# Mixture-of-experts stage: a large and a small expert run as a pair, gate and up of both, then down of both

## The chip, the cores and the metric

One core of one Trainium2 chip runs the whole program. The metric is the device time of one execution in microseconds (us). TensorE (PE) multiplies, VectorE (DVE) and ScalarE (ACT) work on the results, GpSimd (POOL) does little here, SyncE (SP) issues the transfers from HBM, and DMA engines carry them. Every engine takes its own instructions in a written order and waits for the others through semaphores.

## The reference

Two layers of mixers and feed-forward over 256 context and 256 latent tokens of width 1024. The change lies in the feed-forward of the second layer, where each latent token goes to the best two of eight experts:

```python
def swiglu(h, w_gate, w_up, w_down):
    return (jax.nn.silu(h @ w_gate) * (h @ w_up)) @ w_down

def moe_swiglu(h, router_w, w_gate, w_up, w_down):
    logits = (h @ router_w).astype(F32)
    top_v, top_i = lax.top_k(logits, TOP_K)
    top_w = jax.nn.softmax(top_v, axis=-1)
    combine = jnp.sum(jax.nn.one_hot(top_i, N_EXPERTS, dtype=F32) * top_w[..., None], axis=-2)
    out = jnp.zeros(h.shape[:-1] + (w_down.shape[-1],), h.dtype)
    for e in range(N_EXPERTS):
        out = out + combine[..., e:e + 1].astype(h.dtype) * swiglu(h, w_gate[e], w_up[e], w_down[e])
    return out
```

D_MODEL is 1024, D_FF is 2816, all weights are float32: 33 MB (of 1,048,576 bytes) for one expert, 264 for the eight.

## The kernel before

The experts are sorted by the number of their tokens and paired, a large one (up to 128 tokens) with a small one (up to 64): slots 0 and 1, 2 and 3, and so on. An expert that has more tokens than its slot holds is finished by a path behind a branch at the end, which does not run here.

`gather` (L1145) picks the tokens of both experts of a pair by a matmul with a one-hot matrix `oh` and writes `xg` for the large and `xs` for the small one. `pick` (L1136) makes that matrix for the next pair. `scatter_rows` (L1160) turns it for the way back, and `scatter` (L1296) scales one half of an expert's output (`y`, L1300 on ACT and L1301 on DVE), multiplies it with the turned matrix and adds it to the stream `xl` (L1309). The scatter of the second half (`late`) is put off into the expert that follows.

`expert` (L1175) is the large one. Its weights come as 33 loads of 1 MB each, 22 for gate and up in six groups `g`, 11 for down. A weight tile is split into a high and a low part (`split`, L346): ACT writes `whi` (L352), DVE writes `wlo` (L353) from it; two pieces per load, three pairs of buffers. Three matmuls, high with high, high with the low part of the tokens, low with high (L1197 to L1199 for gate and up, L1233 to L1235 for down), stand for one in full precision. The activation of a group (L1202, L1203) is transposed on PE (L1208) in the middle of the next group. `expert64` (L1240) is the small one: its weights are not split, and two halves of the columns go through the array side by side (L1254). Its activation (L1260 on ACT, L1261 on DVE) is transposed (L1266) and copied (L1268, ACT); down is L1290. Four of the next pair's gathers and more stand between its down matmuls.

The loop at the end calls `expert(0)`, `expert64(1)`, `expert(2)` and so on, each with gate and up and then down. Loads are issued by SP in the program's order, as buffers come free; there are ten of them (three in `wpool`, four in `mo`, three of the freed tiles `own` and `whole`). The framework's scheduler sets the written order of each engine from the program's order, its priorities (splits have a high one) and the dependences. PSUM is cut into pools: `pj` three buffers, `pm` three, `po` and `pa` one each. Gate and up of the large expert take `po` and `pa` in even groups and `pj` in odd ones, the small one takes `pj`; down accumulates in two buffers of `pm`, from which transposes, gathers and scatters are served too.

The entries of `PLAN` that matter: `sg` (group after which the scatter rows are made), `tt` and `td` (where in the next group, and in down, a transpose is called), `pk` (after which group `pick` is called), `gd` (first down load with a gather), `sd` (down load after which the first half is scattered).

Of the kernel before, what the change touches and what calls it, by code (L numbers as in the profile page):

```python
# [83 lines left out]
def host_layout(x, c, ctx, c_ctx, ada_w, ada_b, mix_norm_w, ffn_norm_w, w_in, hg_lb_logits, hg_norm_w,  # L84
# [97 lines left out]
    "ff": (1, 1),  # L182
    "sg": 1,
    "tt": 2,
    "td": 2,
    "slots": (3, 5, 8),
    "pk": 3,
    "gd": 1,
    "sd": 8,
    "dv": ([], [4, 5, 6, 7, 8, 9, 10, 11, 12, 13, 14, 15, 16, 17, 18]),  # L190
# [8 lines left out]
def tile_kernel(ctx: ExitStack, tc: tile.TileContext, xT, cT, cR, ada_w, w_in, w_br, w_out, ffn_gu, ffn_d, router,  # L199
# [975 lines left out]
    def expert(e, oh, st, choose, early):  # L1175
        pr, ee = divmod(e, 2)
        at_ = home_of(e)
        if ee:
            return expert64(e, at_, oh, st, choose, early)
        xv = [xg[:, s_] for s_ in range(2)]  # L1180
        aT, turn_ = [], []
        for g in range(6):
# [3 lines left out]
            for u in range(2):  # L1186
                ps = pj() if g % 2 else pt(("po", "pa")[u], 1)
                for c in range(8 // kc):
                    n = 4 * g + 2 * u + c if g < 5 else 20 + u
                    raw = load(moe[at_, n]).rearrange("p (k c) -> p k c", k=kc)  # L1190
                    for k0 in range(0, kc, kc // 2):
                        if turn_ and 4 * (kc * c + k0) >= kc * PLAN["tt"]:
                            turn_.pop()()
                        hi, lo = split(raw[:, k0:k0 + kc // 2], (kc // 2, w))
                        for k in range(kc // 2):
                            kk = kc * c + k0 + k
                            T.matmul(ps[:, :w], xv[0][:, kk], hi[:, k], start=kk == 0, stop=False)  # L1197
                            T.matmul(ps[:, :w], xv[1][:, kk], hi[:, k], start=False, stop=False)  # L1198
                            T.matmul(ps[:, :w], xv[0][:, kk], lo[:, k], start=False, stop=kk == 7)  # L1199
# [15 lines left out]
            if g == PLAN["pk"]:  # L1215
                choose()
            if g == PLAN["sg"]:
                if late:
                    late.pop()()
                st.update(zip(("ws", "oT"), scatter_rows(pr, oh)))  # L1220
        pd = [pm(), pm()]
        for c in range(11):
            raw = load(moe[at_, 22 + c]).rearrange("p (k c) -> p k c", k=4)
            early(c - PLAN["gd"])
            for k in range(4):
                h_, kk = DOWN[4 * c + k]
                if turn_ and 4 * c + k == 2 * PLAN["td"]:
                    turn_.pop()()
                if k % 2 == 0:
                    hi, lo = split(raw[:, k:k + 2], (2, 512))  # L1230
                ahi, alo = (x[:, kk % 4] for x in aT[kk // 4])
# [4 lines left out]
            if c == PLAN["sd"]:  # L1236
                scatter(e, 0, pd[0], st["ws"], st["oT"])
        late.append(lambda: scatter(e, 1, pd[1], st["ws"], st["oT"]))

    def expert64(e, at_, oh, st, choose, early):  # L1240


        aT, turn_ = {}, []
        for g in range(6):
# [3 lines left out]
            for u in range(2):  # L1248
                for c in range(8 // kc):
# [7 lines left out]
                    if turn_:  # L1257
                        turn_.pop()()
# [15 lines left out]
            if g == PLAN["pk"]:  # L1274
                choose()
            if g == PLAN["sg"] and late:
# [3 lines left out]
        pd = [pm(), pm()]  # L1280
        for c in range(11):
            raw = load(moe[at_, 22 + c]).rearrange("p (k c) -> p k c", k=4)
            early(c - PLAN["gd"])
            for k in range(4):
                h_, kk = DOWN[4 * c + k]
                if turn_ and c == 1:
                    turn_.pop()()
# [4 lines left out]
            if c == PLAN["sd"]:  # L1292
                scatter(e, 0, pd[0], st["ws"], st["oT"])
        late.append(lambda: scatter(e, 1, pd[1], st["ws"], st["oT"]))
# [26 lines left out]
    late, ohs = [], [pick(0)]  # L1321
    for k in range(KD):
        gather(k, ohs[0], True)
    for pr in range(4):
        st = {}
        for ee in range(2):
            def choose():
                if ee and pr < 3:
                    ohs.append(pick(pr + 1))

            def ahead(k):
                if ee and pr < 3 and 0 <= k < KD:
                    gather(k, ohs[pr + 1], False)

            expert(2 * pr + ee, ohs[pr], st, choose, ahead)
    late.pop()()
# [109 lines left out]
```

## Time and profile before

| what | us |
|---|---|
| median of 3 runs (2147.19 to 2152.62) | 2149.67 |
| profiled execution | 2153.76 |
| its span on the core | 2151.9 |
| PE busy in the span | 2065.4 |
| DVE busy | 1304.0 |
| ACT busy | 926.7 |

All durations of instructions come from the one profiled execution. A matmul's row lasts longer than the step to the next matmul, because matmuls overlap; a step is read from two starts. The expert stage begins with the first large matmul at 1449.8 us and reaches to 2144 us, and a pair takes about 175 us. In the windows below, 1716.4 to 1763.6 us is gate and up of the second small expert, and 1763.6 to 1790.4 us its down.

### The profile page before, as it was taken

How to read it: one execution, taken by the hardware profiler on the slowest of the kernel's cores; microseconds unless marked ns; L12 is line 12 of the kernel's file. 1: busy time of each engine (PE TensorE's matmuls, PEld its weight loads, DVE VectorE, ACT ScalarE, POOL GpSimd, SP SyncE). 2: the span in 40 equal slices, each digit the busy share in tenths (PEclk: the TensorE clock that was granted, in tenths of full speed). 3: DMA queues.
4: the chain of work that ended last, by engine and by line, in shares of the span. 5: the costliest groups of instructions: out<-in, count | busy, mean ns of one | idle time of the engine just before them, and what ended most of it. 6: DMA issues, size and time to landing. Idle time of an engine off the chain costs nothing.

```text
span 2151.9 us, 34449 instructions
## 1 busy us (share of the span) xinstructions
PE 2065.4 (96%) x13828; PEld 1580.3 (73%) x13828; DVE 1304.0 (61%) x2362; ACT 926.7 (43%) x1423; POOL 35.3 (2%) x101
## 2 busy tenths in 40 slices
PE   6999999999999999999999999989999999999997
PEld 3777777777867878887778878878757856865863
DVE  7677456664455468634777777669618806915931
ACT  3653233322334222223755443448527616815731
POOL 0001000010000000000000000000000000000000
PEclk9999999999999999999999999989999999999999
DMA  8341413112263346421333222469999999999996
GB/s 322 128 157 61 172 64 118 40 61 79 100 233 118 113 163 243 157 67 61 126 128 118 99 102 80 147 245 335 365 422 420 385 419 416 371 397 420 375 392 247
DMA packets 66983, 455.46 MB, mean 212 GB/s; under 512 B 7680, under 2 KB 8192, under 8 KB 13952
## 3 DMA queue, kind: packets, MB, share of 16 engines
q1 hardware_dynamic: 64224, 447.78, 53.9%
q10 hardware_dynamic: 2592, 5.41, 0.8%
q8 instruction: 111, 1.82, 0.3%
q14 instruction: 56, 0.46, 0.1%
HBM read 452.11 MB, written 1.05 MB: 211 GB/s over the span
## 4 chain that ended last, share of the span: by engine, by line
PE 90%; DVE 4%; ACT 3%; DMA 2%; issue 1%; SPq 0%; DVEq 0%; ACTq 0%
PE pj L359 15%; PE pj L361 15%; PE pj L360 15%; PE pj L1254 7%; PE pm L1290 4%; PE pm L1235 2%; PE pm L1233 2%; PE pm L1234 2%; PE pj L1197 2%; PE pj L1198 2%; PE pj L1199 2%; PE pm L596 1%; PE pa L803 1%; PE pm L379 1%; PE po L1199 1%; PE po L1197 1%
## 5 line engine op out<-in xcount | busy, mean ns | idle before, releaser
L352 ACT ACTIVATE whi<-raw 128x1024 fp32r<-128x1024 f32 (+3 forms) x442 | 436.4, 993 | 579.4 <-PE pj L360 504.9
L353 DVE TENSOR_TENSOR wlo<-raw,whi 128x1024 fp32r<-128x1024 f32 (+3 forms) x442 | 497.8, 1140 | 214.6 <-ACT whi L352 203.5
L359 PE MATMUL pj<-hhi,whi 128*128 128x512 f32 (+1 forms) x1216 | 452.0, 373 | 9.9 <-ACT hhi L488 9.0
L361 PE MATMUL pj<-hhi,wlo 128*128 128x512 f32 (+1 forms) x1216 | 450.7, 371 | 0.4 <-DVE wlo L353 0.4
L360 PE MATMUL pj<-hlo,whi 128*128 128x512 f32 (+1 forms) x1216 | 449.7, 370 | 0.2 <-DVE hlo L489 0.2
L359 PEld LDWEIGHTS pj<-hhi,whi 128*128 128x128 f32 x1216 | 230.1, 189 | 51.9 <-ACT hhi L488 11.8
L361 PEld LDWEIGHTS pj<-hhi,wlo 128*128 128x128 f32 x1216 | 229.9, 189 | 40.6 <-issue 5.4
L360 PEld LDWEIGHTS pj<-hlo,whi 128*128 128x128 f32 x1216 | 230.3, 189 | 39.3 <-issue 3.0
L1254 PE MATMUL pj<-raw,whole 128*64 128x256 f32 (+1 forms) x1088 | 114.4, 362 | 0.0
L1261 DVE TENSOR_TENSOR act<-act,pj 128x256 f32<-128x256 f32 (+1 forms) x24 | 9.6, 399 | 156.6 <-ACT act L1260 156.6
L1254 PEld LDWEIGHTS pj<-raw,whole 128*64 128x64 f32 x1088 | 73.5, 137 | 33.2 <-issue 2.2
L1260 ACT ACTIVATE act<-pj 128x256 f32<-128x256 f32 (+1 forms) x24 | 8.8, 367 | 144.2 <-PE pj L1254 144.2
L359 PE MATMUL pj<-yhi,whi 128*128 128x512 f32 (+1 forms) x192 | 66.8, 350 | 3.4 <-ACT yhi L514 3.1
L361 PE MATMUL pj<-ahi,wlo 128*128 128x512 f32 x176 | 69.3, 394 | 0.5 <-DVE wlo L353 0.5
L359 PE MATMUL pj<-ahi,whi 128*128 128x512 f32 x176 | 69.0, 392 | 0.0
L1233 PE MATMUL pm<-whi,ahi 128*128 128x512 f32 x176 | 69.0, 392 | 0.0
L1198 PE MATMUL pj<-whi,xg 128*128 128x512 f32 (+1 forms) x192 | 68.9, 359 | 0.0
L360 PE MATMUL pj<-alo,whi 128*128 128x512 f32 x176 | 68.6, 390 | 0.0
L1234 PE MATMUL pm<-whi,alo 128*128 128x512 f32 x176 | 68.6, 390 | 0.0
L1197 PE MATMUL pj<-whi,xg 128*128 128x512 f32 (+1 forms) x192 | 68.4, 356 | 0.2 <-ACT whi L352 0.2
L1235 PE MATMUL pm<-wlo,ahi 128*128 128x512 f32 x176 | 68.2, 390 | 0.0
L1199 PE MATMUL pj<-wlo,xg 128*128 128x512 f32 (+1 forms) x192 | 68.0, 354 | 0.0
(362 smaller groups left out, 3620.0 us busy)
## 6 DMA issues: line engine op xcount, KB each, us to landing
raw<-in_moe_dram SPq DMA_DIRECT2D x185, 1024.0 KB, 8.8
raw<-in_w_in_dram SPq DMA_DIRECT2D x58, 1024.0 KB, 4.8
own<-in_moe_dram SPq DMA_DIRECT2D x53, 1024.0 KB, 8.9
raw<-in_ada_w_dram SPq DMA_DIRECT2D x44, 1024.0 KB, 4.9
whole<-in_moe_dram SPq DMA_DIRECT2D x26, 1024.0 KB, 8.1
raw<-in_ffn_gu_dram SPq DMA_DIRECT2D x22, 1024.0 KB, 4.9
raw<-in_w_br_dram SPq DMA_DIRECT2D x12, 1024.0 KB, 4.8
raw<-in_ffn_d_dram SPq DMA_DIRECT2D x16, 704.0 KB, 4.1
```

Source lines behind the costliest of these rows:

```text
L352: S.activation(hi, src, AF.Copy)
L353: V.tensor_tensor(lo, src, hi.bitcast(F32), ALU.subtract)
L359: T.matmul(ps, whi(k), hhi(k), start=first and k == 0, stop=False)
L360: T.matmul(ps, whi(k), hlo(k), start=False, stop=False)
L361: T.matmul(ps, wlo(k), hhi(k), start=False, stop=last and k == n - 1)
L1197: T.matmul(ps[:, :w], xv[0][:, kk], hi[:, k], start=kk == 0, stop=False)
L1198: T.matmul(ps[:, :w], xv[1][:, kk], hi[:, k], start=False, stop=False)
L1199: T.matmul(ps[:, :w], xv[0][:, kk], lo[:, k], start=False, stop=kk == 7)
L1233: T.matmul(pd[h_], ahi, hi[:, k % 2], start=first, stop=False)
L1234: T.matmul(pd[h_], alo, hi[:, k % 2], start=False, stop=False)
L1235: T.matmul(pd[h_], ahi, lo[:, k % 2], start=False, stop=last)
L1254: T.matmul(ps[64 * h_:64 * h_ + 64, u, :hw], xs[:, kk], raw[:, k, h_ * hw:(h_ + 1) * hw], start=u + kk == 0, stop=u == 1 and kk == 7, tile ...
```

## The change

Both functions become generators. `expert` and `expert64` no longer run to their end: they give back control after each group of gate and up and after each load of down. A new function `pair` calls them in turn. In pair 0 a string gives the order of the groups: three large, six small, three large; in the other pairs six large, then six small. After that come the 11 down loads of the large expert, then the 11 of the small one. The list of transposes to be made, `turn_`, is now one for both. Down accumulates in `po` and `pj` (large) and `pa` and `pj` (small) instead of `pm`. The late scatter of the large expert falls into small down, that of the small expert still into the next pair's gate and up. `pk` counts the groups of both experts, and `td` is gone.

```diff
     "tt": 2,
-    "td": 2,
     "slots": (3, 5, 8),
-    "pk": 3,
+    "pk": 8,
     "gd": 1,
     "sd": 8,
+    "first": "BBBSSSSSSBBB",
...
-    def expert(e, oh, st, choose, early):
-        pr, ee = divmod(e, 2)
+    turn_, late = [], []
+
+    def do_turn():
+        if turn_:
+            turn_.pop()()
+
+    def expert(e):
...
-                        if turn_ and 4 * (kc * c + k0) >= kc * PLAN["tt"]:
-                            turn_.pop()()
+                        if 4 * (kc * c + k0) >= kc * PLAN["tt"]:
+                            do_turn()
...
-            if g == PLAN["pk"]:
-                choose()
-            if g == PLAN["sg"]:
-                if late:
-                    late.pop()()
-                st.update(zip(("ws", "oT"), scatter_rows(pr, oh)))
-        pd = [pm(), pm()]
+            yield
+        pd = [None, None]
         for c in range(11):
             raw = load(moe[at_, 22 + c]).rearrange("p (k c) -> p k c", k=4)
-            early(c - PLAN["gd"])
             for k in range(4):
                 h_, kk = DOWN[4 * c + k]
-                if turn_ and 4 * c + k == 2 * PLAN["td"]:
-                    turn_.pop()()
+                if c == 1 and k == 0:
+                    do_turn()
...
+                if pd[h_] is None:
+                    pd[h_] = pj() if h_ else pt("po", 1)
...
-            if c == PLAN["sd"]:
-                scatter(e, 0, pd[0], st["ws"], st["oT"])
-        late.append(lambda: scatter(e, 1, pd[1], st["ws"], st["oT"]))
+            yield pd
...
-    def expert64(e, at_, oh, st, choose, early):
+    def expert64(e):
...
-                    if turn_:
-                        turn_.pop()()
+                    do_turn()
...
         for c in range(11):
             raw = load(moe[at_, 22 + c]).rearrange("p (k c) -> p k c", k=4)
-            early(c - PLAN["gd"])
+            do_turn()
             for k in range(4):
                 h_, kk = DOWN[4 * c + k]
-                if turn_ and c == 1:
-                    turn_.pop()()
+                if pd[h_] is None:
+                    pd[h_] = pj() if h_ else pt("pa", 1)
...
+    def pair(pr):
+
+        both = expert(2 * pr), expert64(2 * pr + 1)
+        for n, who in enumerate(PLAN["first"] if pr == 0 else "B" * 6 + "S" * 6):
+            next(both["BS".index(who)])
+            if n == PLAN["sg"]:
+                if late:
+                    scatter(*late.pop())
+                rows = scatter_rows(pr, ohs[pr])
+            if n == PLAN["pk"] and pr < 3:
+                ohs.append(pick(pr + 1))
+        for ee in range(2):
+            e = 2 * pr + ee
+            for c in range(11):
+                pd = next(both[ee])
+                if c == PLAN["sg"] and late:
+                    scatter(*late.pop())
+                if c == PLAN["sd"]:
+                    scatter(e, 0, pd[0], *rows)
+                if ee and pr < 3 and 0 <= c - PLAN["gd"] < KD:
+                    gather(c - PLAN["gd"], ohs[pr + 1], False)
+            late.append((e, 1, pd[1], *rows))
...
     for pr in range(4):
-        st = {}
-        for ee in range(2):
-            def choose():
-                if ee and pr < 3:
-                    ohs.append(pick(pr + 1))
-
-            def ahead(k):
-                if ee and pr < 3 and 0 <= k < KD:
-                    gather(k, ohs[pr + 1], False)
-
-            expert(2 * pr + ee, ohs[pr], st, choose, ahead)
-    late.pop()()
+        pair(pr)
+    scatter(*late.pop())
```

In the kernel after, the lines of the large expert are L1202 to L1204 (gate and up), L1213 (its transpose) and L1234 to L1236 (down); of the small one L1254 as before, L1259 (activation), L1265 (transpose), L1267 (copy) and L1286 (down). In the scalings L1294 stands for L1300.

ACT, at the end of the second pair's small gate and up (`act` is the activation, `whole` holds the copies of the transposes, `x` and `xg` belong to the gathers). Before:

```order
L1268 ACTIVATE whole<-pm_15674 128x256
L1260 ACTIVATE act_15696<-pj_15655 128x128
L1156 ACTIVATE x_15714<-pm_15709,mods_145,coef_149 128x128
L1156 ACTIVATE whole<-pm_15709,mods_145,coef_149 128x64
L1157 ACTIVATE xg_13119<-x_15714 128x128
L1268 ACTIVATE whole<-pm_15719 128x128
L1156 ACTIVATE x_15732<-pm_15727,mods_145,coef_149 128x128
```

Now, at the same place:

```order
L1267 ACTIVATE whole<-pm_15399 128x256
L1259 ACTIVATE act_15421<-pj_15381 128x128
L1267 ACTIVATE whole<-pm_15449 128x128
L352 ACTIVATE whi_15426<-raw_15424 128x1024
L352 ACTIVATE whi_15437<-raw_15424 128x1024
L352 ACTIVATE whi_15452<-raw_15447 128x1024
```

The splits of the large expert's down weights follow the small expert's last copy directly, where the gathers stood.

PE at the same place. Before, small gate and up is followed by small down and gathers, with the last transpose among them:

```order
L1254 MATMUL pj_15655<-raw_15656,whole 64x128 x16
L1254 MATMUL pj_15655<-raw_15678,whole 64x128 x16
L1290 MATMUL pm_15699<-raw_15701,whole 64x512 x4
L1148 MATMUL pm_15709<-oh_15604,hn_2117_13065 128x192 x2
L1148 MATMUL pm_15709<-oh_15604,hn_2118_13066 128x192 x2
L1266 MATMUL pm_15719<-cc,act_15696 128x128
L1290 MATMUL pm_15699<-raw_15707,whole 64x512 x4
```

Now it is followed by the transpose and then by large down:

```order
L1254 MATMUL pj_15381<-own,whole 64x128 x16
L1254 MATMUL pj_15381<-raw_15403,whole 64x128 x16
L1265 MATMUL pm_15449<-cc,act_15378 128x128
L1234 MATMUL po_15430<-whi_15426,ahi_14638 128x512
L1235 MATMUL po_15430<-whi_15426,alo_14639 128x512
L1236 MATMUL po_15430<-wlo_15427,ahi_14638 128x512
```

The transpose stands right behind its group, and the first large matmuls need the split parts `whi` and `wlo`.

ACT at the end of the last pair's small gate and up, where L1279 (now L1275) has a table of functions loaded. Before:

```order
L1260 ACTIVATE act_18368<-pj_18327 128x128
ACT_TABLE_LOAD
L1279 ACTIVATE most_18371<-act_18368 128x1
L1268 ACTIVATE whole<-pm_18382 128x128
L1300 ACTIVATE y_18429<-pm_18373,ws_17415 128x512
```

Now:

```order
L1259 ACTIVATE act_18093<-pj_18052 128x128
ACT_TABLE_LOAD
L1275 ACTIVATE most_18357<-act_18093 128x1
L352 ACTIVATE whi_18098<-raw_18096 128x1024
L352 ACTIVATE whi_18109<-raw_18096 128x1024
L1267 ACTIVATE whole<-pm_18120 128x128
L352 ACTIVATE whi_18123<-own 128x1024
```

Two splits stand ahead of the last copy here, behind the table and L1275.

## Rows read from the trace of the kernel before

**Rows 1.** The page's busy time, share and instructions of PE; shares of the ending chain:

```profile
PE 2065.4 (96%) x13828; PEld 1580.3 (73%) x13828; DVE 1304.0 (61%) x2362; ACT 926.7 (43%) x1423; POOL 35.3 (2%) x101
...
PE 90%; DVE 4%; ACT 3%; DMA 2%; issue 1%; SPq 0%; DVEq 0%; ACTq 0%
```

**Rows 2.** Windows: length, busy time (instructions) PE, PEld, DVE, ACT, POOL, PEclk, DMA share, GB/s:

```profile
1449.80:1619.40 169.60, 165.73 (x993) 118.70 (x992) 96.53 (x116) 88.61 (x122) 0.00 (x0) 0.99 0.94 369
1619.40:1792.10 172.70, 165.69 (x1001) 119.09 (x1001) 98.88 (x117) 89.36 (x120) 0.00 (x0) 1.00 1.00 409
...
1716.40:1763.60 47.20, 42.50 (x405) 28.19 (x406) 4.52 (x10) 4.53 (x11) 0.00 (x0) 1.00 1.00 408
1763.60:1790.40 26.80, 26.70 (x131) 10.55 (x125) 5.04 (x14) 8.75 (x27) 0.00 (x0) 1.00 1.01 420
```

**Rows 3.** Waits of PE, 1450 to 2144 us: total, times, longest us:

```profile
PE pm L1266 <- DVE act L1261: 16.0, 17, 0.9
PE po L1197 <- ACT whi L352: 5.2, 3, 1.7
PE po L1199 <- DVE wlo L353: 1.6, 3, 0.5
...
```

**Rows 4.** Timeline, first small to large turn: start, length, engine, line, operation, idle before:

```profile
1615.80 1.89 PE L1290 MATMUL pm<-whole 128*64 128x512 f32 x8
...
1617.73 0.69 ACT L1300 ACTIVATE y<-pm,ws 128x512 fp32r<-128x512 f32 x1 [5.67 <-PE pm L1290]
1618.32 2.94 ACT L352 ACTIVATE whi<-raw 128x1024 fp32r<-128x1024 f32 x3
...
1619.40 3.49 DVE L353 TENSOR_TENSOR wlo<-raw,whi 128x1024 fp32r<-128x1024 f32 x3 [0.19 <-ACT whi L352]
...
1619.42 0.50 PE L1197 MATMUL po<-whi,xg 128*128 128x512 f32 x1 [1.73 <-ACT whi L352]
...
1620.68 0.50 PE L1199 MATMUL po<-wlo,xg 128*128 128x512 f32 x1 [0.53 <-DVE wlo L353]
...
1621.01 0.39 PE L1197 MATMUL po<-whi,xg 128*128 128x512 f32 x1
...
1621.24 0.39 PE L1198 MATMUL po<-whi,xg 128*128 128x512 f32 x1
```

**Rows 5.** Timeline, end of the last small gate and up:

```profile
2107.65 0.42 DVE L1261 TENSOR_TENSOR act<-act,pj 128x256 f32<-128x256 f32 x1 [8.01 <-ACT act L1260]
2108.12 0.44 PE L1266 MATMUL pm<-cc,act 128*128 128x128 f32 x2 [0.94 <-DVE act L1261]
...
2112.03 1.89 PE L1290 MATMUL pm<-own,whole 128*64 128x512 f32 x8
2112.25 0.28 ACT L1260 ACTIVATE act<-pj 128x128 f32<-128x128 f32 x1 [3.27 <-PE pj L1254]
2112.56 0.29 DVE L1261 TENSOR_TENSOR act<-act,pj 128x128 f32<-128x128 f32 x1 [4.49 <-ACT act L1260]
2113.84 0.20 ACT L1279 ACTIVATE most<-act 128x1 f32<-128x1 f32 x1 [1.31 <-DVE act L1261]
2113.85 0.33 PE L1266 MATMUL pm<-cc,act 128*128 128x128 f32 x1
...
2114.22 0.28 ACT L1268 ACTIVATE whole<-pm 128x128 f32<-128x128 f32 x1 [0.17 <-PE pm L1266]
```

**Rows 6.** Windows behind the three turns (columns as in rows 2):

```profile
1793.40:1796.80 3.40, 3.38 (x8) 2.70 (x9) 2.84 (x3) 1.66 (x2) 0.00 (x0) 0.50 1.01 419
1967.40:1970.80 3.40, 3.01 (x7) 2.44 (x8) 2.85 (x4) 2.02 (x3) 0.00 (x0) 0.51 1.01 419
1617.50:1624.50 7.00, 4.74 (x21) 3.50 (x20) 5.76 (x6) 5.78 (x7) 0.00 (x0) 1.00 1.01 421
```

**Rows 7.** DMA issues, 1546 to 1617 us; the last number is us to landing:

```profile
raw<-in_moe_dram SPq DMA_DIRECT2D x22, 1024.0 KB, 14.4
```

More of the change, by code (lines that the diff above doesn't have):

```diff
@@ L182 @@
     "ff": (1, 1),
+    "tt": 2,
+    "slots": (3, 5, 8),
+    "pk": 8,
     "sg": 1,
-    "tt": 2,
-    "td": 2,
-    "slots": (3, 5, 8),
-    "pk": 3,
     "gd": 1,
     "sd": 8,
+    "first": "BBBSSSSSSBBB",
     "dv": ([], [4, 5, 6, 7, 8, 9, 10, 11, 12, 13, 14, 15, 16, 17, 18]),
@@ L1173, in scatter_rows @@
         return ws, oT
-    def expert(e, oh, st, choose, early):
-        pr, ee = divmod(e, 2)
+    turn_, late = [], []
[3 more added lines that the diff above has]
+    def expert(e):
         at_ = home_of(e)
-        if ee:
-            return expert64(e, at_, oh, st, choose, early)
         xv = [xg[:, s_] for s_ in range(2)]
-        aT, turn_ = [], []
+        aT = []
         for g in range(6):
@@ L1235, in expert @@
                 T.matmul(pd[h_], ahi, lo[:, k % 2], start=False, stop=last)
-            if c == PLAN["sd"]:
-                scatter(e, 0, pd[0], st["ws"], st["oT"])
-        late.append(lambda: scatter(e, 1, pd[1], st["ws"], st["oT"]))
-    def expert64(e, at_, oh, st, choose, early):
-        aT, turn_ = {}, []
+            yield pd
+    def expert64(e):
+        at_ = home_of(e)
+        aT = {}
         for g in range(6):
@@ L1273, in expert64 @@
             turn_.append(turned)
-            if g == PLAN["pk"]:
-                choose()
-            if g == PLAN["sg"] and late:
-                late.pop()()
+            yield
         if e == NE - 1:
             S.activation(mt((1,), "most"), a[:, 0:1], AF.Exp, scale=0.0)
-        pd = [pm(), pm()]
+        pd = [None, None]
         for c in range(11):
             raw = load(moe[at_, 22 + c]).rearrange("p (k c) -> p k c", k=4)
-            early(c - PLAN["gd"])
+            do_turn()
             for k in range(4):
                 h_, kk = DOWN[4 * c + k]
-                if turn_ and c == 1:
-                    turn_.pop()()
+                if pd[h_] is None:
+                    pd[h_] = pj() if h_ else pt("pa", 1)
                 r = kk % 2
@@ L1291, in expert64 @@
                          tile_position=(0, 64 * r), skip_group_check=True)
-            if c == PLAN["sd"]:
-                scatter(e, 0, pd[0], st["ws"], st["oT"])
-        late.append(lambda: scatter(e, 1, pd[1], st["ws"], st["oT"]))
+            yield pd
     def scatter(e, h_, pd, ws, oT):
@@ L1320, in tile_kernel @@
     norm = Norm(256, lambda: pt("po", 1))
-    late, ohs = [], [pick(0)]
+    def pair(pr):
[19 more added lines that the diff above has]
+            late.append((e, 1, pd[1], *rows))
+    ohs = [pick(0)]
     for k in range(KD):
@@ L1324, in tile_kernel @@
     for pr in range(4):
-        st = {}
-        for ee in range(2):
-            def choose():
-                if ee and pr < 3:
-                    ohs.append(pick(pr + 1))
-            def ahead(k):
-                if ee and pr < 3 and 0 <= k < KD:
-                    gather(k, ohs[pr + 1], False)
-            expert(2 * pr + ee, ohs[pr], st, choose, ahead)
-    late.pop()()
+        pair(pr)
+    scatter(*late.pop())
     more["own"] = []
```

## The prediction

> **What bounds the kernel now.** I read the page first, then the change's own stage (the experts, from 1450 us to the end at 2144 us) pair by pair, then what TensorE (PE) waits for there, then two short stretches of the timeline. The page says that PE is busy for 96% of the span and carries 90% of the chain that ended last [rows 1]. In the expert stage the first two pairs take 169.6 and 172.7 us with PE busy for 165.7 and 165.7 of them [rows 2]. The same rows show a DMA share of 0.94 and 1.00, so from them alone either could be the bound. The list of PE's waits decides: it has 7 rows for the whole stage, the largest are given, and none names a DMA [rows 3]. The weights always lie there when PE comes to them. So PE's own order is the bound, its work is fixed, and the change can move the time only through the gaps between pieces of that work. There are few: 17 waits of at most 0.9 us for the activation of a small group (16.0 us together), and 3 places where PE begins a large expert straight after a small one, 5.2 us for the high halves and 1.6 us for the low halves of the first weights [rows 3].
>
> **Why those 3 places cost.** [rows 4] is one of them. ScalarE (ACT) makes the high half of the split weights and VectorE (DVE) the low half. Small experts need no split, so both have time to spare, but ACT takes its instructions in their written order, and the first split stands behind the scaling of the small expert's output (L1300), which waits for the last small matmul. L1300 starts at 1617.73, the first split at 1618.32, and the first large matmul at 1619.42, after 1.73 us of idling. The third matmul needs the low half and starts at 1620.68, 1.26 after the first, where two ordinary steps take 0.46 (1621.01 to 1621.24 is one step, 0.23). So a place costs 1.73 + 0.80 = 2.5 us, or 1.73 + 0.53 = 2.26 if only the idle time of the rows is counted.
>
> **The clock.** After two of these places the granted clock stands at 0.50 and 0.51, which is the 1.2 GHz level, for the 3.4 us shown; after the one in [rows 4] it stayed at 1.00 [rows 6]. Ahead of each fall the engine had done the same: idled 1.73 us, run two matmuls, idled 0.53. In 3.4 us at half clock 1.7 us of work are lost. I price a fall at 1.7 us with two chances in three.
>
> **The change part by part.** The work is the same: matmuls, splits, loads, gathers, scatters. What moves is the order.
>
> Small gate and up now stand ahead of the large expert's down (in the first pair, ahead of the second half of its gate and up). A small-to-large turn inside the pair is new, four in all, and the turn to the next pair stays, three, written as before (the scaling of the small output, then the splits). In the first three new turns ACT's row is activation of group 5, copy of its transpose, then the splits, with nothing of the splits ahead. In PE's row the transpose of group 5 stands directly ahead of the first large matmul. Before, small down matmuls and gathers stood between them, and the copy had time.
>
> The price of a new turn comes from [rows 5], where the last small group ends in the kernel before. PE could go on at 2112.03. The activation L1260 starts at 2112.25 and takes 0.28; the product L1261 runs from 2112.56 to 2112.85; a transpose follows 0.05 later, as at 2108.12 behind a product that ended at 2108.07; so 2112.90. The copy L1268 starts 0.37 behind its transpose (2113.85 to 2114.22) and takes 0.28: 2113.55. From the start of a split to the matmul are 1.10 us (1618.32 to 1619.42): 2114.65. That is 2.62 us, less 0.33 for the transpose, which is work in both kernels: 2.29. With the 0.80 for the low half a turn costs 3.1 us.
>
> In the last pair two splits are written ahead of the copy, but behind the loading of another function table and L1279. In [rows 5] L1279 starts at 2113.84 and takes 0.20: the split starts at 2114.04, the matmul at 2115.14, 3.11 us after 2112.03; less 0.33, plus 0.80, 3.6 us. Before, this stood beside eight small down matmuls and delayed nothing but a transpose.
>
> The waits for small activations hardly change. In the first pair a transpose of the large expert falls into the small stretch and shifts the others by one weight tile, so that eight further small matmul rows stand ahead of four transposes; at the fifth and in all later pairs the transposes stand directly behind their group as before. So 16 remain of 17: 0.9 us back.
>
> With one answer, nothing: the scatter of the large expert's second half and the gathers now both lie in small down, 26.8 us long with ACT busy for 8.75 and DVE for 5.04 of it [rows 2], so both find room; the large output's accumulators move from the pool of three PSUM buffers to others, which come free in time; loads keep their number, only their order follows the program. On SyncE's queue the small expert's address is read after 12 loads instead of 33, and the number has been there since the routing. The wait at each new turn holds up, behind it on ACT, the splits alone, and PE waits for these: that is already the price. If data were late at a turn it would cost more. In small gate and up 22 loads are used in 47.2 us; at 408 GB/s one takes 1.05 MB / 408 GB/s = 2.6 us, so the lead shrinks by some 10 us; with large down behind it instead of small down the lead recovers sooner than before. So no cost.
>
> **The sum.** 3 x 3.1 + 3.6 - 0.9 = 12.0 us of gaps, and 4 x 2/3 x 1.7 = 4.5 us of clock: 16.5 us. The profiled execution took 2153.76 us, 4.1 above the median of 2149.67; on its side that would be 2170.3, on the median's 2166.2. I take the median's: **2166 us, 0.8% slower**. Lower bound: four turns at 2.26, 0.9 back, no fall of the clock in any turn and so 2 x 1.7 back: +4.7, 2154. Upper bound: 12.9 of turns with nothing back, all seven turns with a fall (five more, 8.5): +21.4, 2171; the runs before reach 3 us above their median, so 2174.
>
> **Rivals.** About 0.3% (6.4 us) is what a measurement of this kernel can tell from no change.
> *Cheap turns.* The turns cost idle time alone and the clock holds in all: 2155. For it: the turn in [rows 4] kept its clock. Against it: the new turns idle longer than those that lost it.
> *The small waits go.* Before, the two down accumulators held two of the three buffers in which transposes are written. If the 17 waits came from that shortage, they go with it, 16.0 us back against 12.9 and 4.5: 2151, no change. Against it: the rows name the product L1261 as what PE waited for, and during gate and up no down accumulator is held except while its scatter is late. The Trainium skill, Perfetto Trace Analysis, section Identifying Performance Opportunities, says that a gap which repeats on the engine that should be saturated can mean too little SBUF or PSUM for the next tile; by that rule the sum would be this rival's, by the rows mine.
> *The loads bind after all (faster).* If PE's busy time hid lateness of loads, a mix of heavy and light stretches would keep the queue full from the first pair on; there its share is 0.94 of 169.6 us, so 10 us could come back, with the turns covered by waits for data that exist anyway: 2140. It decides from the point where a load lands after its first use. A load lands 14.4 us after its issue in the small stretch [rows 7]; its buffer, one of ten, is used again after ten uses of some 2.1 us (47.2 us for 22), 21 us. So 7 us are in hand, and no PE wait names a DMA. The same section of the Trainium skill advises to interleave stretches with different limits; it speaks for this change, but here the trace shows one limit in both.
> *Deep falls.* After a turn the clock falls twice over, in all seven: 12.0 + 14 x 1.7 - 3.4 = +32, 2182. No row shows two falls in a row in this stage.
>
> **How the numbers follow.** Forecast 0.74 (2157 to 2174), cheap turns 0.09, small waits gone 0.06, loads bind 0.05, deep falls 0.06. Slower by over 0.3%: 0.74 + 0.06 = 0.80; within 0.3%: 0.09 + 0.06 = 0.15; faster: 0.05. The range 2154 to 2174 takes in the forecast and most of the cheap turns, and leaves out some 0.2.
>
> **What would show it.** Right: PE's waits list four turns into the large expert inside the pairs, each with over 2 us idle ahead of the high half and 0.5 ahead of the low half, beside the three old ones; small waits near 15 us; clock at half after four to five of seven turns; pairs some 3 to 5 us longer, the last too. Wrong: if the splits have run ahead of the copy, if PE waits for a DMA in either kernel, or if the small waits have gone.

## The result and the profile after

The changed kernel takes 2166.4 us (median of 4 runs, 2162.9 to 2167.19) beside 2148.43 us (median of 4, 2146.45 to 2152.62) of the kernel before: 1.0074 times as long, 95% interval 1.006 to 1.0088, or 12.9 to 18.9 us more. The forecast was 2166 us. The profiled execution took 2165.68 us, its span 2163.8.

Where the time lies is seen first pair by pair. The windows run from the first large matmul of a pair to that of the next, the last one to the end of the closing norm (columns as in rows 2). The kernel before:

```profile
1449.60:1619.42 169.82, 165.94 (x995) 118.90 (x994) 96.74 (x116) 88.83 (x122) 0.00 (x0) 0.99 0.94 369
1619.42:1792.16 172.74, 165.69 (x1001) 119.09 (x1001) 98.87 (x118) 89.40 (x120) 0.00 (x0) 1.00 1.00 409
1792.16:1966.53 174.37, 167.31 (x1002) 120.30 (x1002) 98.99 (x118) 89.38 (x120) 0.00 (x0) 0.99 0.99 397
1966.53:2141.40 174.87, 167.10 (x992) 120.20 (x993) 97.37 (x109) 84.34 (x103) 0.00 (x0) 0.99 0.91 363
```

And after:

```profile
1446.43:1617.22 170.79, 165.41 (x996) 117.81 (x994) 96.18 (x118) 88.63 (x123) 0.00 (x0) 1.00 0.96 390
1617.22:1796.13 178.91, 169.41 (x1001) 121.40 (x1002) 99.40 (x118) 89.54 (x120) 0.00 (x0) 0.98 0.97 387
1796.13:1973.50 177.37, 167.88 (x1001) 120.18 (x1001) 99.32 (x118) 89.55 (x120) 0.00 (x0) 0.99 0.98 391
1973.50:2153.40 179.90, 169.48 (x992) 120.72 (x993) 97.62 (x109) 84.34 (x103) 0.00 (x0) 0.98 0.85 337
```

The pairs are longer by 1.0, 6.2, 3.0 and 5.0 us, 15.2 together; the prediction had looked for some 3 to 5 in each. The page counts 13828 matmuls in both kernels, so no work was added.

PE's waits in this stage of the changed kernel, the counterpart of [rows 3] (engine, tile, line, releaser: total, times, longest us):

```profile
PE pm L1265 <- DVE act L1260: 17.8, 20, 0.9
PE po L1202 <- ACT whi L352: 5.2, 3, 1.7
PE po L1234 <- ACT whi L352: 4.4, 3, 1.8
PE po L1236 <- DVE wlo L353: 1.6, 3, 0.5
PE po L1204 <- DVE wlo L353: 1.6, 3, 0.5
PE pj L1202 <- ACT whi L352: 1.5, 2, 1.3
PE pj L1204 <- DVE wlo L353: 0.5, 1, 0.5
...
```

The three old turns stand there unchanged (5.2 us for high halves, 1.6 us for low ones). The four new ones are the rows L1234, L1236 and `pj`, three in front of large down and one in front of the second half of expert 0's gate and up. The first row holds two things: 16 waits of 0.94 us, one fewer than in [rows 3], and four of 0.70 us for the last small transpose, which belong to the new turns. No row names a DMA.

A new turn in the timeline, the counterpart of [rows 5] (start, length, engine, line, operation, idle before):

```profile
1731.08 0.28 ACT L1259 ACTIVATE act<-pj 128x128 f32<-128x128 f32 x1 [3.27 <-PE pj L1254]
1731.39 0.29 DVE L1260 TENSOR_TENSOR act<-act,pj 128x128 f32<-128x128 f32 x1 [4.50 <-ACT act L1259]
...
1731.73 0.33 PE L1265 MATMUL pm<-cc,act 128*128 128x128 f32 x1 [0.70 <-DVE act L1260]
1732.10 0.28 ACT L1267 ACTIVATE whole<-pm 128x128 f32<-128x128 f32 x1 [0.74 <-PE pm L1265]
1732.27 2.94 ACT L352 ACTIVATE whi<-raw 128x1024 fp32r<-128x1024 f32 x3
...
1733.37 0.50 PE L1234 MATMUL po<-whi,ahi 128*128 128x512 f32 x1 [1.31 <-ACT whi L352]
...
1734.63 0.79 PE L1236 MATMUL po<-wlo,ahi 128*128 128x512 f32 x1 [0.53 <-DVE wlo L353]
...
```

Read it downward: activation, product, transpose, copy, and only then the splits, though the first of these weights had landed 9 us before, at 1723.26. PE idles 0.70, 1.31 and 0.53 us, 2.54 in all; the last pair has 1.81 in place of 1.31. The matmul at 1734.63 already lasts 0.79 us instead of 0.50.

The windows behind all seven turns, in order of time (the counterpart of [rows 6]):

```profile
1527.90:1531.30 3.40, 2.87 (x13) 2.35 (x13) 3.40 (x4) 2.67 (x4) 0.00 (x0) 1.00 1.01 419
1618.50:1621.90 3.40, 3.40 (x8) 2.72 (x9) 2.84 (x3) 1.62 (x2) 0.00 (x0) 0.50 0.99 381
1734.60:1738.00 3.40, 3.37 (x8) 2.69 (x9) 2.84 (x3) 1.67 (x2) 0.00 (x0) 0.50 1.01 422
1797.10:1800.50 3.40, 3.11 (x14) 2.57 (x15) 3.40 (x4) 2.67 (x3) 0.00 (x0) 1.00 0.96 381
1912.10:1915.50 3.40, 3.40 (x9) 2.63 (x10) 2.90 (x3) 1.50 (x2) 0.00 (x0) 0.50 1.02 424
1974.50:1977.90 3.40, 3.13 (x14) 2.60 (x15) 3.40 (x4) 2.67 (x3) 0.00 (x0) 1.00 0.97 347
2089.50:2092.90 3.40, 3.07 (x7) 2.48 (x8) 2.84 (x4) 2.14 (x3) 0.00 (x0) 0.51 1.02 424
```

Four of seven fell to 0.50 (the 1.2 GHz level) for the 3.4 us shown: three new turns (1734.6, 1912.1, 2089.5) and one old one (1618.5). In the same time PE starts 7 to 9 matmuls instead of 13 or 14. The kernel before had two falls behind three turns [rows 6]. The 24th matmul behind the first large one starts 7.8 to 8.0 us after it where the clock fell and 6.4 us where it held: a fall costs 1.4 to 1.6 us.

### The profile page after: what moved, and what is told of

Same layout as the page of the kernel before. It is cut to its first block, busy times and chain, and to the rows that moved or that the text cites. A ratio compares the mean times of both kernels' runs of the same rounds, so it can differ in the third digit from the quotient of the medians.

```text
span 2163.8 us, 34449 instructions
## 1 busy us (share of the span) xinstructions
PE 2069.3 (96%) x13828; PEld 1580.8 (73%) x13828; DVE 1304.1 (60%) x2362; ACT 926.5 (43%) x1423; POOL 35.4 (2%) x101
## 4 chain that ended last, share of the span: by engine, by line
PE 90%; DVE 4%; ACT 3%; issue 1%; DMA 1%; DVEq 0%; SPq 0%; ACTq 0%
PE pj L359 15%; PE pj L361 15%; PE pj L360 15%; PE pj L1254 7%; PE pa L1286 2%; PE pj L1286 2%; PE pj L1204 2%; PE pj L1202 2%; PE pj L1203 2%; PE pm L596 1%; PE pa L803 1%; DVE wlo L353 1%; PE pm L379 1%; PE po L1204 1%; ACT whi L352 1%
## 5 line engine op out<-in xcount | busy, mean ns | idle before, releaser
L1254 PE MATMUL pj<-raw,whole 128*64 128x256 f32 (+1 forms) x1056 | 113.0, 365 | 0.0
L1254 PEld LDWEIGHTS pj<-raw,whole 128*64 128x64 f32 x1056 | 71.6, 137 | 33.2 <-issue 2.7
L1202 PE MATMUL pj<-whi,xg 128*128 128x512 f32 (+1 forms) x192 | 68.6, 357 | 1.5 <-ACT whi L352 1.5
L1204 PE MATMUL pj<-wlo,xg 128*128 128x512 f32 (+1 forms) x192 | 68.2, 355 | 0.5 <-DVE wlo L353 0.5
L360 PE MATMUL pj<-ylo,whi 128*128 128x512 f32 (+1 forms) x192 | 66.4, 346 | 0.0
L353 DVE TENSOR_TENSOR wlo<-own,whi 128x1024 fp32r<-128x1024 f32 x52 | 62.0, 1221 | 7.2 <-ACT whi L352 5.7
L361 PE MATMUL pj<-yhi,wlo 128*128 128x512 f32 (+1 forms) x192 | 66.2, 345 | 0.0
L1259 ACT ACTIVATE act<-pj 128x256 f32<-128x256 f32 (+1 forms) x24 | 8.8, 367 | 132.7 <-PE pj L1254 132.7
```

The lines of the kernel that those rows point to most:

```text
L353: V.tensor_tensor(lo, src, hi.bitcast(F32), ALU.subtract)
L360: T.matmul(ps, whi(k), hlo(k), start=False, stop=False)
L361: T.matmul(ps, wlo(k), hhi(k), start=False, stop=last and k == n - 1)
L1254: T.matmul(ps[64 * h_:64 * h_ + 64, u, :hw], xs[:, kk], raw[:, k, h_ * hw:(h_ + 1) * hw], start=u + kk == 0, stop=u == 1 and kk == 7, tile ...
```

## Experiments

All were timed beside the kernel before on the same chip. "Stage" is the length of the expert stage in the profiled execution, from the first large matmul to the last matmul of the closing norm: 691.9 us before, 707.1 us after. It leaves out the part ahead, which by itself ends up to 8 us earlier or later from one profiled execution to another.

**The order undone.** The changed kernel's pools and generators, but each expert runs whole, and the late scatters stand again in the gate and up that follows:

```diff
-        for n, who in enumerate(PLAN["first"] if pr == 0 else "B" * 6 + "S" * 6):
-            next(both["BS".index(who)])
...
         for ee in range(2):
...
+            for n in range(6):
+                next(both[ee])
...
```

The transpose at the end of a small gate and up was kept behind the first down matmuls, as before.

> The changed kernel with the order of the groups undone: each expert runs gate and up and then down, the large one first, with the pools of the changed kernel kept. Theory (the time comes from the four new turns from small to large work): they are gone, the three old turns and 17 waits of about 0.9 us for small activations stay, so 2149 us, +-3, and 0.992 of the changed kernel. Rival 1 (the moved accumulators or other pool edits cost it): the time stays at 2166. Rival 2 (the small waits are a shortage of PSUM buffers, which the pools of the changed kernel lift): the 17 waits are gone and the time is near 2149 - 16 = 2133.

Measured: 2150.32 us beside 2150.32, ratio 1.0001 (0.9992 to 1.001); stage 691.2. The waits are those of [rows 3]:

```profile
PE pm L1265 <- DVE act L1260: 16.0, 17, 0.9
PE po L1202 <- ACT whi L352: 5.2, 3, 1.7
PE po L1204 <- DVE wlo L353: 1.6, 3, 0.5
...
```

So the order alone costs the time, and the other pools neither cost nor give anything. The 17 small waits are there with the transposes in a pool that no down accumulator shares, so no accumulator that holds PSUM causes them. (The Trainium skill, Perfetto Trace Analysis, section Identifying Performance Opportunities, says that a repeating gap can mean such a shortage; here it did not.)

**The inner turns hidden.** The paired order, but the first three pieces of the large weights are loaded and split ahead of the last small group:

```diff
+    def ahead(e, n):
+        piece(e, n, 0), piece(e, n, 2), piece(e, n + 1, 0)
...
+            if n == (8 if pr == 0 else 11):
+                ahead(2 * pr, 12 if pr == 0 else 22)
```

`piece` makes a split once and keeps it. The large expert's first step was kept behind the last small matmul on PE.

> The changed kernel, but at the four turns inside the pairs the first three pieces of the large weights are loaded and split ahead of the last small group, and the large expert's first step stands behind the last small matmul on TensorE as before. Theory (the turn costs because the splits wait on ScalarE behind the activation and the copy of the last small group): the idle stretches of these turns go (3 x 2.54 + 3.04 = 10.7 us), and with them the falls of the clock behind them (3 x 1.7 = 5.1 us): 2166 - 16 = 2150 us (2147 to 2154). Rival 1 (the splits delay the activations of the last small group by as much): about 2161. Rival 2 (the cause lies elsewhere, in loads or in matmuls that got slower): 2166.

Measured: 2148.9 us beside 2150.32, ratio 1.0 (0.9989 to 1.0011); stage 689.8, with falls behind two of the old turns and none behind an inner one. The first rows that are left:

```profile
PE pm L1281 <- DVE act L1276: 15.0, 16, 0.9
PE po L1218 <- ACT whi L352: 5.2, 3, 1.7
PE po L1220 <- DVE wlo L353: 1.6, 3, 0.5
...
```

The rows of the inner turns are gone, and with them the whole loss. That the splits stood behind the last copy on ACT was the cause, not the pairing as such.

**The idle time filled, the waits kept.** Five extra matmuls, whose result nobody uses, behind the last small transpose of each inner turn:

```diff
+            for q in range(5):
+                T.matmul(spare, xg[:, 0, 0], xg[:, 0, 0:4].rearrange("p k c -> p (k c)"), start=True, stop=True)
```

> The changed kernel with five extra matmuls of 128 x 512, whose result nobody uses, behind the last small transpose at each of the four turns inside the pairs; they take about 5 x 0.23 = 1.15 us and lie in the 1.31 us in which TensorE idles there. All waits stay. Theory (a turn costs its idle time and, separately, the fall of the clock that follows): the idle stretches ahead of the high halves are filled, the falls at 0.50 behind these turns vanish or get fewer than the three seen, and the time drops by 0 to 5 us, 2161 to 2166. Rival 1 (a fall costs nothing because the loads or the splits set the pace in those 3.4 us anyway): the falls vanish and the time stays at 2166. Rival 2 (the falls don't come from the idle stretch): three or more falls stay and the time is 2166 to 2169.

Measured: 2163.6 us (2161.45 to 2165.06), ratio 1.006 (1.0047 to 1.0074); stage 703.4, 3.6 less than without them. The windows behind the four inner turns:

```profile
1531.30:1534.70 3.40, 2.88 (x14) 2.38 (x14) 3.40 (x4) 2.68 (x4) 0.00 (x0) 1.00 1.02 422
1736.40:1739.80 3.40, 3.38 (x15) 2.82 (x16) 3.38 (x3) 2.69 (x3) 0.00 (x0) 1.00 1.01 419
1913.80:1917.20 3.40, 3.38 (x15) 2.77 (x16) 3.37 (x3) 2.64 (x3) 0.00 (x0) 1.00 1.01 422
2091.70:2095.10 3.40, 3.37 (x15) 2.81 (x16) 3.38 (x3) 2.85 (x3) 0.00 (x0) 1.00 1.02 424
```

No fall is left there. The profile's other two falls lie behind old turns (1798.5 and 1976.0), so there are two instead of four, worth 2 x 1.5 = 3.0 us of the 3.6. (The closing norm, at full clock here, gives 0.9 more, and a start of the stage at the lower clock takes 0.4.) In the six profiles that keep these turns as they are (the changed kernel and the runs with nine and eight buffers, expert 0 in one part, the small waits alone and the paired load order below) 18 of 24 fell. So the idle stretch ahead of the high half brings the fall, and the fall is a cost of its own. By the medians alone (2163.6 and 2166.4, whose intervals overlap) the gain would not be certain.

**More turns.** The first pair in alternation:

```diff
-    "first": "BBBSSSSSSBBB",
+    "first": "BSBSBSBSBSBS",
```

> The changed kernel with the first pair's gate and up in turns, one part of the large expert and one of the small in alternation, so that this pair has five more turns from small to large work. Theory (each turn has its price): five turns at 1.5 to 3.2 us, part of them followed by a fall at 1.7 us, less some of the five small waits of this pair: 2166 + 8 to 20 = 2174 to 2186 us, all of it in the first pair. Rival (mixing heavy and light stretches evens out the loads): the first pair gets shorter than the 174 us of the changed kernel and the time drops below 2166.

Measured: 2175.62 us (2173.73 to 2179.33), ratio 1.0126 (1.011 to 1.0142); stage 715.8, and 8.4 of the 8.7 us that it has more lie in the first pair (179.2 instead of 170.8 us). The size was as expected, the way there was not: PE's waits show idle of over 1 us at only one of this pair's inner turns (1.42 us ahead of L1202), because the scheduler moved most splits ahead. The clock fell at 1545.5, for twice the usual time, and at 1562.5, where the changed kernel has no fall in this pair: 3 x 1.5 = 4.5 us. Another 1.0 is the start of the stage, whose first five steps took 2.19 us at the lower clock instead of 1.17. The rest is not assigned.

**The small waits alone.** The small transposes one weight tile later:

```diff
-                    do_turn()
+                    with tc.issue_after(getattr(at_end, "ins", at_end)):
+                        do_turn()
```

> The changed kernel with one order edit: the transposes of a small group stand behind the first weight tile of the next group instead of directly behind their own group. Theory (the 16 small waits come from the order: TensorE stands still while ScalarE and VectorE make the activation, 0.9 us each): 16 x 0.94 = 15.0 us go, 2166 - 15 = 2151 us (2147 to 2154); the seven turns stay as they are. Rival (the waits are a shortage of PSUM buffers): the transposes only wait elsewhere, as does the next group, and the time stays at 2166.

Measured: 2144.23 us beside 2148.4, ratio 0.9983 (0.9973 to 0.9992), some 20 us less than the changed kernel and below the range that was expected; stage 688.0, 19.0 less.

```profile
PE po L1202 <- ACT whi L352: 5.2, 3, 1.7
...
PE po L1234 <- ACT whi L352: 4.4, 3, 1.8
PE pm L1266 <- DVE act L1261: 2.8, 4, 0.7
...
```

All 16 waits are gone and the turns stand as they were (the four 0.70 us are theirs). From start to start of its matmuls a wait costs 1.01 us, a little more than its row of 0.94 (in the changed kernel the transpose starts 1.32 us after the matmul ahead of it where PE waits, 0.31 where it doesn't). So the waits give 16.2 us, one fall fewer (three) 1.5 and the closing norm, at full clock here, 0.9: 18.6 of the 19.0. No pool was touched, so the waits were of order, not of PSUM. One line of order thus outweighs what the change costs.

**Fewer load buffers.** `slots` with two entries instead of three makes nine, with one entry eight (the list of freed tiles was cut to match):

```diff
-    "slots": (3, 5, 8),
+    "slots": (3, 5),
```

> The changed kernel with nine load buffers instead of ten. Theory (the loads have about 7 us in hand in the small stretch and one buffer less takes about 2.1 to 2.6 us of it): no wait for a DMA in the expert stage, 2166 us, +-2. Rival (the loads bind after all and the longer small stretch of the pair has used up the lead): waits for DMA appear in the small gate and up of each pair, 2 us or more a pair, 2174 or more.

> The changed kernel with eight load buffers instead of ten. Theory (7 us in hand with ten; nine showed no wait for a DMA, each buffer less takes about 2.1 us): some 2.7 us are left, no wait for a DMA, 2166 us +-3. Rival (the lead is smaller than that): waits for a DMA in the small gate and up of the pairs, 2170 or more.

Measured: nine 2165.6 us, ratio 1.0083 (1.007 to 1.0096), stage 707.1, level with ten. Eight: 2171.27 us (2165.97 to 2175.87), ratio 1.0103 (1.0082 to 1.0123), stage 711.7. Neither list of waits names a DMA. The expectation of 2166 +-3 for eight was missed, though its interval overlaps that of the changed kernel (1.006 to 1.0088). Its profile shows six falls instead of four (3.0 us), one small wait more (1.0) and a start at the lower clock (first five steps 2.19 us instead of 1.17), which together make up the 4.6 us that its stage is longer; why the falls came with eight buffers is open. Loads did not bind in the changed kernel.

**Expert 0 in one part.** The string in pair 0 becomes six large and six small groups:

```diff
-    "first": "BBBSSSSSSBBB",
+    "first": "BBBBBBSSSSSS",
```

> The changed kernel with expert 0's gate and up in one part: in the first pair, too, the small gate and up stand between the large gate and up and the large down. Theory (the two parts change only where a turn stands and how many small transposes are covered): the turn of the first pair moves to the large down at the same 2.5 us; four more small waits of 0.94 us appear in the first pair, since no large transpose shifts the small ones there: 2166 + 3.8 = 2170 us (2167 to 2172). Rival (cutting expert 0 in two is what costs, by two turns where one would do): 2163 or less.

Measured: 2164.62 us, ratio 1.0077 (1.0063 to 1.009); stage 708.0. The turn moved to large down as expected. The four extra small waits did not come, and the time stayed under the 2167 to 2172 expected with them (20 entries, 17.8 us, as in the changed kernel), since here too a transpose of the large expert falls behind the first small tile and shifts the others. The two parts of expert 0 are worth nothing that can be measured.

**All gaps at once, paired and in sequence.** Both edits, splits ahead at every turn and lagging transposes, on the paired order and on the old one:

```diff
+            if n == (8 if pr == 0 else 11):
+                ahead(2 * pr, 12 if pr == 0 else 22)
...
+                if ee and c == 9 and pr < 3:
+                    ahead(2 * pr + 2, 0)
...
-                    do_turn()
+                    with tc.issue_after(getattr(at_end, "ins", at_end)):
+                        do_turn()
```

> The changed kernel with both: at all seven turns the first three pieces of the large weights are loaded and split ahead of the last small group, and the small transposes stand behind the first weight tile of the next group. Theory: 16 small waits of 0.94 us (15.0), four turns inside the pairs (10.7) and three between pairs (3 x 2.26 = 6.8) go, and four falls at 1.7 (6.8): 2166 - 39 = 2127 us (2122 to 2134), faster than the kernel before. Rival (what is taken away at one place comes back as a wait for the splits or the loads at the next, now that the slack is used): 2140 or more, with waits for splits or a DMA in the list.

> The order of the kernel before (each expert gate and up, then down), with the splits of the first three large pieces ahead of the last small group at its three turns, and the small transposes one weight tile later, those in small down too. Theory (the pairing is worth nothing by itself; it only adds turns): once the turns are hidden, both orders cost the same, 2127 us +-4, level with the paired kernel that has the same two edits. Rival 1 (pairing evens out the loads and is worth something once the gaps are gone): this one is slower than that one by 3 us or more, with waits for a DMA in its list. Rival 2 (each hidden turn still costs something): this one, with three turns instead of seven, is 2 us or more faster.

Measured: paired 2130.2 us (2126.06 to 2137.74), ratio 0.9916 (0.9899 to 0.9932); in sequence 2126.93 us (2121.58 to 2132.89), ratio 0.9904 (0.9889 to 0.9919). Both beat both kernels, the better by some 22 us against the kernel before and 40 against the changed one. Their intervals overlap, so neither order is shown to be better. The profiled stages differ more, 678.1 us paired and 668.7 in sequence: the paired one waits 3.9 us longer for a DMA, and its profile has two falls and a closing norm at half clock, which the other's has not. The waits of the paired one:

```profile
PE pj L1270 <- DMA raw<-in_moe_dram: 7.6, 3, 3.0
PE pj L1270 <- ACT whi L352: 1.4, 1, 1.4
...
```

Of the one in sequence:

```profile
PE pj L1305 <- DMA own<-in_moe_dram: 2.4, 2, 1.9
PE pj L1305 <- DMA raw<-in_moe_dram: 2.2, 4, 0.8
...
PE pa L1305 <- DMA own<-in_moe_dram: 0.5, 1, 0.5
...
```

The old rows are all gone, and for the first time a DMA stands there, 5.1 us in sequence and 9.0 paired (the row that names `whi` is a small matmul, which uses no split: it starts at 2055.28, 0.14 us after a load has landed at 2055.14, as the three others start 0.13 to 0.14 us behind a landing, so its 1.4 us are a fourth of these). Middle pairs of the one in sequence (columns as in rows 2):

```profile
1608.00:1774.00 166.00, 164.69 (x1003) 119.13 (x1001) 99.53 (x117) 89.71 (x120) 0.00 (x0) 1.00 1.01 417
1774.00:1942.00 168.00, 165.59 (x1007) 119.30 (x1003) 101.10 (x119) 91.27 (x122) 0.00 (x0) 1.00 1.01 416
```

A pair has 66 loads of 1.0486 MB, 69.2 MB; at 417 GB/s that is 166 us, as long as PE is busy. So once the gaps are out, loads and PE stand level.

**The load order mended.** In both, the small weights that the early loads overtake are to be loaded first (the upper part is in the paired kernel alone):

```diff
+                raw_of(2 * pr + 1, 20), raw_of(2 * pr + 1, 21)
                 ahead(2 * pr, 12 if pr == 0 else 22)
...
+                    raw_of(e, 31), raw_of(e, 32)
                     ahead(2 * pr + 2, 0)
```

> The paired kernel with hidden turns and lagging small transposes (x5_all_lag), with one more edit: the loads of the last small weights are issued ahead of the loads of the large pieces that are split early, so that the order on the load queue is again that of use. Theory (its waits for a DMA, 2.7, 3.0, 1.9 and 1.4 us at the last small group of each pair, come from that overtaking alone): they go, 9.0 us, and two falls of the clock with them, 1.6 us each: 2130 - 12 = 2118 us (2114 to 2124). Rival (the loads are the bound once the gaps are gone): the waits move to another small tile and the time stays near 2130.

> The sequential kernel with hidden turns and lagging small transposes (x6_seq_lag), with the same edit of the load order. Theory (overtaking): its 5.1 us of waits for a DMA go, 2127 - 5 = 2122 us (2117 to 2126), level with the paired kernel with the same edits: the expert stages would then be 662.7 - 9.0 - 3.2 = 650.5 us paired and 654.6 - 5.1 = 649.5 us in sequence. Rival (the pairing evens out the loads): DMA waits stay here and not in the paired one, which is then 3 us or more faster.

Measured: paired 2144.19 us, ratio 0.9978 (0.9967 to 0.9989), stage 688.0; in sequence 2131.87 us, ratio 0.9919 (0.9905 to 0.9934), stage 671.5. Both expectations fell, since the edit did more than was meant. With the small loads first, the scheduler put the splits back behind the last copy, as the paired kernel's timeline shows:

```profile
1722.59 0.28 ACT L1284 ACTIVATE whole<-pm 128x128 f32<-128x128 f32 x1 [0.74 <-PE pm L1282]
1722.77 1.05 ACT L352 ACTIVATE whi<-raw 128x1024 fp32r<-128x1024 f32 x1
```

All seven turns came back (three in sequence), and the waits for a DMA went but for 0.2 us. What the overtaking costs with hidden turns stays open. But the two are now the same work with the same lag, and differ by four inner turns: 688.0 - 671.5 = 16.5 us of stage. The profile in sequence has lost 1.0 us at the start of the stage (first five steps 2.19 us, paired 1.17) and 1.1 in the closing norm (3.08 us from its first start to its last, paired 1.96) to the lower clock, so the order is worth 18.6. Three falls, in the paired profile alone, take 4.3 of it; 14.3 are left, 3.6 a turn. The third pair, without a fall in either, shows one turn by itself, paired in the first row and in sequence in the second (columns as in rows 2):

```profile
1785.09:1955.83 170.74, 165.94 (x1002) 119.05 (x1002) 99.21 (x118) 89.50 (x120) 0.00 (x0) 1.00 1.00 406
1784.76:1951.76 167.00, 164.74 (x1001) 119.17 (x1002) 98.90 (x118) 89.45 (x120) 0.00 (x0) 1.00 1.01 416
```

That is 3.7 us, 0.6 more than the 3.1 of the turn itself (worked out below); 0.4 of it lie in the pair's other transposes, which stand beside other matmuls in this order.

## Why the prediction was right

**The bound.** PE's order was the limit, and no wait for a DMA came up in either kernel, nor with eight or nine buffers. That step held. What it did not see is how near the second limit is: in sequence with the gaps gone the stage is 668.7 us long, 23 us shorter than before, and there loads and PE stand level.

**The turns.** Four new ones, where they were expected, by the mechanism expected: undone, they go with the order; with the splits ahead, they go without it. Each was priced at 3.1 us, and it cost that, though two terms of the price were off and cancelled. PE's rows show 2.54 us of idle time, but idle time is counted from the end of the last small matmul's row, and these rows overlap: in [rows 5] the next matmul had started at 2112.03, 0.17 us before that row ended (2108.49 + 3.71 = 2112.20, first row; the second is that of the changed kernel).

```profile
2108.49 3.71 PE L1254 MATMUL pj<-raw,whole 128*64 128x128 f32 x64
1729.12 1.92 PE L1254 MATMUL pj<-raw,whole 128*64 128x128 f32 x32
```

So up to the transpose a turn takes 0.17 + 0.70 = 0.87 us (second row: from 0.17 us ahead of its end, 1731.04, to 1731.73), as worked out. From the transpose to the first large matmul it takes 1.64 (1731.73 to 1733.37), where the sum had 0.37 + 0.28 + 1.10 = 1.75: the split started 0.17 us behind the start of the copy (1732.10 to 1732.27), and the copy's full 0.28 had been charged. Then 0.80 for the low half (1733.37 to 1734.63 less 0.46). For the transpose the sum took off 0.33, the length of its row; in the kernel before, the next matmul starts 0.20 us behind it (0.26 in the last pair), and that is all that it cost there. 0.87 + 1.64 + 0.80 - 0.20 = 3.1 us; in the last pair 0.87 + 2.14 + 0.80 - 0.26 = 3.55, priced at 3.6.

**The small waits.** 16 of 17 stayed, as worked out, and came from the order; the one that went gave back 1.0 us by its starts, for the 0.9 of the forecast. The rival "the small waits go" fell with the first experiment.

**The clock.** The forecast had four more chances of two in three at 1.7 us, 4.5 us. The profiled executions had two more falls (four of seven turns against two of three) at 1.4 to 1.6, about 3.1 in all. The size was a little high. The chance was near for the new turns, with 2.54 us of idle time: three of four fell here, 18 of 24 over the six profiles above. Of the old ones, with 2.26, one in three fell here and two in three before, 15 of 36 over the twelve profiles that have them; a fall more or fewer between two profiles is no finding. Which turn falls is not to be foretold from its idle time.

**The sum.** Pair by pair: 3.1 - 1.0 = 2.1 us in pair 0, of which the kernel before gives back 1.0, because its first five steps took 2.18 us at the lower clock and here 1.17, so 1.1; measured 1.0. Pair 1: 3.1 + 2 falls = 6.2; measured 6.2. Pair 2: 3.1 and as many falls as before; measured 3.0. Pair 3: 3.6, as many falls as before, and 0.9 in the closing norm, most of which ran at half clock in the changed kernel (second row, the first is that of the kernel before; from its first start to its last 2.85 us, before 1.96):

```profile
2139.50 2.34 PE L450 MATMUL po<-sq,oned 128*128 128x256 f32 x8 [0.73 <-ACT sq L447]
2150.62 3.48 PE L450 MATMUL po<-sq,oned 128*128 128x256 f32 x8 [0.73 <-ACT sq L447]
```

That is 4.5; measured 5.0, and where the rest lies is not known. Together 14.9 of 15.2. The gaps were right: 11.9 us against the forecast's 12.0. The clock behind the turns was 3.1 against 4.5. The two terms that the forecast did not have, the start and the closing norm, nearly cancel (1.0 back, 0.9 more). The forecast's 16.5 lies within the interval of the medians (12.9 to 18.9): the hit to 0.4 us is partly luck, the mechanism is not.

**The rivals.** "Cheap turns" is out: falls came and cost time, and filling the idle stretch took them away. "Loads bind after all" would have needed waits for a DMA; they come only with all gaps closed, in a stage 3% (in sequence) to 4% (paired) shorter. "Deep falls" did not show: two falls of double length in the alternating kernel (1545.5 and 2095.0), one fall a turn at most in the changed one.

## What to carry to other kernels

An engine that takes its instructions in order makes early work late when it stands behind something that depends on another engine's last result: where light work (no splits) is followed by heavy work, write the heavy work's preparation ahead of the last light group, and count the turns before adding some. A turn with 2.5 us of idle time on PE cost up to 1.6 us more behind it, through the clock. Before reordering to balance engines against loads, ask what PE waits for: here the waits were all of order, a one-line lag took out 16 of them, and once the gaps were closed the two orders could not be told apart by their times.

## What the runs showed of the hardware beyond what was expected

- On ACT the next instruction starts before the one ahead has ended: 0.17 us after the start of a copy of 0.28 us, in the changed kernel and in the one with the load order mended (1722.59 to 1722.77, 0.18).
- The granted clock fell behind idle stretches that were split by work: 0.70, a transpose, 1.31, two matmuls, 0.53. With five matmuls in the middle stretch (leaving 0.70, 0.17 and 0.53, in the last pair 0.65 for 0.17) it fell behind none of four.
- The same turn in the same place falls in one kernel and not in another: behind the turn at about 1527 us the clock held in the changed kernel and fell with the lagging transposes (1528.8) and with eight buffers (1528.9). The clock also differs where nothing was changed: the first five steps of the stage took 1.17 to 2.19 us, the closing norm 1.96 or 2.85 to 3.16 from its first start to its last.
- The loads of this stage ran at 416 to 417 GB/s over two whole pairs with a DMA share of 1.01; the kernel before had 409 in its fullest pair.
